# Linear attention with ReLU features: loads issued ahead of the stores in one DMA queue, larger runs, and one order of work to the end

## The chip, the core and the metric

The kernel runs on one NeuronCore of a Trainium2 chip. Five engines work side by side, each through its own queue in order: TensorE (PE) does matmuls and transposes into PSUM, VectorE (DVE) and ScalarE (ACT) do elementwise work, GpSimd (POOL) issues most DMA transfers here, and SyncE (SP) issues a few. Sixteen DMA engines move the data between HBM and the on-chip SBUF; each transfer is spread over all sixteen, and its semaphore is complete when the last of them has reported. The metric is the device time in microseconds (us) of one execution, the median over several. A profiled execution has a span, from its first instruction to its last, and a somewhat longer time.

## The reference

For each of 8 x 12 = 96 heads, with 512 positions and 64 dimensions, all in fp32:

```python
Q_feat = np.maximum(0, Q)
K_feat = np.maximum(0, K)
KV = np.einsum('bhkd,bhkv->bhdv', K_feat, V)        # 64 x 64 per head
K_sum = np.sum(K_feat, axis=2)
numerator = np.einsum('bhqd,bhdv->bhqv', Q_feat, KV)
denominator = np.einsum('bhqd,bhd->bhq', Q_feat, K_sum)
return numerator / (denominator[:, :, :, None] + 1e-10)
```

Q, K and V hold 12.58 MB each, and so does the result.

## The kernel before, in words

**Tiling.** Heads are taken eight at a time: an "octet" `o`, 12 in all (`NO`). An octet's Q, K, V and result are 1.05 MB each in HBM. K and V of an octet are cut into two groups of four heads, `g = 2*o` and `2*o+1`. Loads through GpSimd cast fp32 to bf16 on the way, so a load writes half of what it reads. Octet 0 comes another way: K and V in fp32 through SP and ACT (lines 124 and 125), Q through GpSimd.

**Buffers.** `k_all`, `v_all` and `q_all` are a ring of six octets (`RING = DELAY + 1 = 6`): octet `o` lies in slot `(o-1) % 6`. A load of octet `o + 6` therefore waits until octet `o` has been used: K by VectorE (line 195), V by VectorE and ScalarE (197, 204, 202), Q by TensorE's transposes (230). Results go into `o_sb`, seven rotating buffers, of which the fp32 K and V of octet 0 take the first two.

**GpSimd's queue.** GpSimd issues its transfers in program order, and a transfer whose wait is not met holds up those behind it. The compiler gives these transfers eight semaphores in turn, so each transfer also waits for the one eight places ahead to land. Before: octets 1 to 6 in three runs of two (`FIRST`), K, then V, then Q; then store 0, store 1, load 7, store 2, load 8, store 3 and so on to store 5, load 11, and stores 6 to 9. The load of octet `o + 6` follows the store of octet `o` in `store` (lines 309 to 311). From octet 9 on (`PAIRS`) K and V come by group, in halves. Stores 10 and 11 go through SP, the last in two halves (lines 301 to 305).

**Work per octet.** `prep(g)` (DVE, lines 195 and 197) and `prep_v` (204 on DVE, 202 on ACT) make ReLU(K) and V masked for their place. `mm_kv` (line 209) sums K-transposed V over 16 matmuls per group, and `evac_kv` (219) copies it to SBUF as `kvd`. `qt` transposes Q on TensorE (230) and applies ReLU (238). `denom` (269, 272, 277, 281) makes the reciprocal of the denominator; `out_t` (260, 262) the numerator, transposed; `back` (287) transposes it back, and `norm` (293) multiplies by the reciprocal into `o_sb`. `idle` (247) is a number of matmuls whose result nobody reads.

**Order of work.** The schedule is written by hand; each engine runs its instructions in the order of the program. For `o` from 0 to 8 an iteration is: K-V matmuls and evacuation of `o`, preparation of group `2o+2`, back and norm of `o-1`, denominators and output of `o`, preparation of `2o+3`, transposed Q of `o+1`. From octet 9 on the order changes: the K-V matmuls of `o+1` and the back of `o` are drawn into iteration `o` (lines 359 to 361), and the last two octets are written out in lines 363 to 388, with some of ScalarE's copies put on VectorE (`share`, and `relu_q` with `nc.vector`).

Of the kernel before, what the change touches and what calls it, by code (L numbers as in the profile page):

```python
# [10 lines left out]
def kernel(  # L11
# [7 lines left out]
    nc = tc.nc  # L19
    B, H, S, D = Q.shape  # L20
    assert D == 64
    P = 128
    D1 = D + 1
# [4 lines left out]
    RQ = S * 8 // P  # L28
    NHG = 4
    U = RQ // 2  # L30
    NG = NH // NHG
    NO = NG // 2
# [3 lines left out]
    fp32 = mybir.dt.float32  # L36
    bf16 = mybir.dt.bfloat16
    Act = mybir.ActivationFunctionType
# [23 lines left out]
    NK = 2  # L62
# [26 lines left out]

    q_sb, k_sb, v_sb = {}, {}, {}  # L90

    PAIRS = NO - 3
    RING = DELAY + 1
    FIRST = (2, 2, 2)
    k_all = consts.tile([P, 2 * RING, R, D], bf16, name="k_all")
    v_all = consts.tile([P, 2 * RING, R, D], bf16, name="v_all")
    q_all = consts.tile([P, RING + 1, U, 2 * D], bf16, name="q_all")
# [6 lines left out]

    def load_kv(X, tile_, first, n):
        to = 2 * ((first // 2 - 1) % RING) + first % 2
        if n == 1:
            nc.gpsimd.dma_start(out=tile_[:, to].rearrange("p r d -> p (r d)"), in_=X[first], single_packet=True)  # L108
            return
        nc.gpsimd.dma_start(out=tile_[:, to:to + n].rearrange("p n r d -> p n (r d)"),  # L110
                            in_=X[first:first + n].rearrange("n p f -> p n f"), single_packet=True)

# [13 lines left out]
    load_q(0)  # L126
    make_identity(nc, ident)

    def load_octet(o, n=1):
        m = 1 if o >= PAIRS else 2 * n  # L130
        for g in range(2 * o, 2 * (o + n), m):
            load_kv(Kr, k_all, g, m)
            load_kv(Vr, v_all, g, m)
        load_q(o, n)

    o = 1
    for n in FIRST:
        load_octet(o, n)
        o += n
    assert o == RING + 1  # L140

    def zero_masks():
        for h in range(NHG):
# [48 lines left out]
    def prep(g):  # L192
        kf[g] = kfp.tile([P, R, 2, D], bf16, name="kf")
        for s in range(2):
            nc.vector.tensor_scalar(kf[g][:, :, s, :], k_sb[g], scalar1=0.0,  # L195
                                    scalar2=mask[:, 0, s:s + 1], op0=Alu.max, op1=Alu.mult)
        nc.vector.tensor_scalar(vo[g % NB][:, :, 0, 2:D + 2], v_sb[g], scalar1=mask[:, 1, 0:1],  # L197
                                scalar2=None, op0=Alu.mult)

    def prep_v(g, eng):  # L200
        if eng is nc.scalar:
            nc.scalar.activation(vo[g % NB][:, :, 1, 2:D + 2], v_sb[g], Act.Copy, scale=mask[:, 1, 1:2])  # L202
        else:
            nc.vector.tensor_scalar(vo[g % NB][:, :, 1, 2:D + 2], v_sb[g], scalar1=mask[:, 1, 1:2],  # L204
                                    scalar2=None, op0=Alu.mult)

    def mm_kv(g):
        for r in range(R):
            nc.tensor.matmul(  # L209
                ps_kv[:, g % 2, 0:2 * (D + 2)].rearrange("p (t d) -> p t d", t=2),  # L210
                kf[g][:, r, :, :].rearrange("p s d -> p (s d)"), vo[g % NB][:, r, :, 1:D4 - 1],
                start=(r == 0), stop=(r == R - 1), skip_group_check=True)


    def evac_kv(o, gs, share=False):
        for s in range(2):
            for c in range(2):
                copy = nc.vector.tensor_copy if share and c == 1 else nc.scalar.copy
                copy(  # L219
                    kvd[o % NK][64 * c:64 * c + 64, 4 * gs.start + s:4 * gs.stop:2,  # L220
                               c * D1:c * D1 + D1].rearrange(
                        "p (g t) d -> p g t d", t=2),
                    ps_kv[64 * s:64 * s + 64, gs, 0:2 * (D + 2)].rearrange(
                        "p g (t d) -> p g t d", t=2)[:, :, :, c:c + D1])


    def transp(o, i):
        ps = pqt.tile([P, U // 2, P], bf16, name="ps_qt")
        for u in range(U // 2):
            nc.tensor.transpose(ps[:, u, :], q_sb[o][:, i * (U // 2) + u, :], ident)  # L230
        return ps

    def relu_q(o, i, ps, eng=None):
        to = qt_sb[o % NZ][:, i * (U // 2):(i + 1) * (U // 2)]
        if eng is nc.vector:
            nc.vector.tensor_scalar(to, ps, scalar1=0.0, scalar2=None, op0=Alu.max)
        else:
            nc.scalar.activation(to, ps, Act.Relu)  # L238

    def qt(o):  # L240
        for i in range(2):
            relu_q(o, i, transp(o, i))


    def idle(n, o):
        for i in range(n):
# [2 lines left out]

    def out_t(o, halves=range(2)):
        if halves[0] == 0:
            ot[o] = otp.tile([P, U, 8, 16], fp32, name="ot_sb")
        q = qt_sb[o % NZ].rearrange("p u (h c) -> p u h c", h=8)
        for j in halves:
# [9 lines left out]
    def denom(o):  # L266
        ps = ps_den[:, 0].rearrange("p (u h c) -> p u h c", u=U, h=8)
        for u in range(U):
            nc.tensor.matmul(ps[:, u], qt_sb[o % NZ][:, u, :], kvd[o % NK][:, :, 0:2 * D1:2 * D1 - 1],  # L269
                             start=True, stop=True, skip_group_check=True)  # L270
        own = rcp.tile([P, U, 8, 2], fp32, name="own")
        nc.vector.scalar_tensor_tensor(
            own.rearrange("p u h c -> p u (h c)"), ps.rearrange("p u h c -> p u (h c)"), 1e-10,
            mask_h.rearrange("p h c -> p (h c)").unsqueeze(1).to_broadcast([P, U, 16]),
            op0=Alu.add, op1=Alu.mult)
        den = rcp.tile([P, RQ], fp32, name="den")
        nc.vector.tensor_reduce(out=den.rearrange("p (u c) -> p u c", c=2),  # L277
                                in_=own.rearrange("p u h c -> p u c h"), op=Alu.add,
                                axis=mybir.AxisListType.X)
        rec[o] = rcp.tile([P, RQ], fp32, name="rec")  # L280
        nc.vector.reciprocal(rec[o], den)
# [15 lines left out]


    def store(o, o_sb):
        Ov = Or[o].rearrange("p (r d) -> p r d", d=D)  # L300
        if o == NO - 1:
            for j in range(2):
                rs = slice(RQ // 2 * j, RQ // 2 * (j + 1))
                nc.sync.dma_start(out=Ov[:, rs], in_=o_sb[:, rs])
            return
        if o >= NO - 2:
            nc.sync.dma_start(out=Ov, in_=o_sb)
            return
# [7 lines left out]
    both = slice(0, 2)  # L316
# [15 lines left out]
    def backs(o):  # L332
        o_sb = out_tile()
        for j in range(2):
            norm(o, j, back(o, j), o_sb)
        store(o, o_sb)

    def kvs(o):
        mm_kv(2 * o)
        mm_kv(2 * o + 1)  # L340
        evac_kv(o, both)

    SAME = NO - 4
    for o in range(NO - 2):
        if 0 < o <= SAME:
            kvs(o)
        prep(2 * o + 2)
        prep_v(2 * o + 2, nc.scalar)  # L350
        if 0 < o <= SAME:
            backs(o - 1)
        denom(o)
        out_t(o)
        prep(2 * o + 3)
        prep_v(2 * o + 3, nc.vector)
        if o >= SAME:
            kvs(o + 1)
        qt(o + 1)
        if o >= SAME:  # L360
            backs(o)

    o = NO - 2
    g = 2 * NO - 2
    prep(g)
    prep_v(g, nc.vector)
    denom(o)
    out_t(o)
    mm_kv(g)
    evac_kv(o + 1, slice(0, 1))  # L370
    prep(g + 1)
    prep_v(g + 1, nc.vector)

    o_sb = out_tile()
    norm(o, 0, back(o, 0), o_sb)
    ps = back(o, 1)
    mm_kv(g + 1)
    evac_kv(o + 1, slice(1, 2), share=True)
    for i in range(2):
        relu_q(o + 1, i, transp(o + 1, i), nc.vector if i == 1 else None)  # L380
    norm(o, 1, ps, o_sb)
    store(o, o_sb)
    idle(5, o + 1)
    out_t(o + 1, (0,))
    denom(o + 1)
    out_t(o + 1, (1,))
    idle(6, o + 1)
    backs(o + 1)
# [1 line left out]
_INS = ['Q', 'K', 'V']  # L390
_OUTS = [((8, 12, 512, 64), 'float32')]
# [25 lines left out]
```

## Time and profile before

| What | Value |
|---|---|
| median of 3 runs | 126.27 us (125.77, 126.27, 126.27) |
| the profiled execution's time | 126.86 us |
| its span | 125.1 us |
| TensorE matmul busy | 86.3 us, 69% of the span |
| VectorE busy | 83.2 us, 67% |
| ScalarE busy | 80.6 us, 64% |
| read from HBM, written | 37.75 MB, 12.58 MB |
| GpSimd's transfers: packets, share of 16 engines' span | 9104, 94.5% |

In the page's second part the span is cut into 40 slices of 3.1 us. A digit is the busy share of a slice in tenths; the DMA row is the mean over the sixteen DMA engines. GB/s counts what is written, so a casting load shows half of what it reads. A line of a timeline holds start, duration, engine, source line, operation, result and operands, and how many instructions stand in it; in brackets the idle time before it and what ended it. "Landing" times are the moments at which the DMA engines reported that their part of a transfer was done, in us from the span's start.

### The profile page before, as it was taken

What the parts mean: (1) busy time and instruction counts of PE and PEld (TensorE: products, weight loads), DVE (VectorE), ACT (ScalarE), POOL (GpSimd) and SP (SyncE); (2) the same over time, 40 slices, a digit from 0 to 9 for tenths busy, and PEclk for the clock granted to TensorE, in tenths of its full rate; (3) what the DMA queues carried; (4) which work ended last, traced back from release to release, by engine and by line L of the source; (5) the groups of instructions that cost most, each with busy time, mean ns of one, the idle gap of its engine ahead of it and who ended that gap; (6) DMA issues with size and microseconds to landing.
All of it is one profiled execution on the core that took longest, in us unless ns stands there. A gap on an engine that the chain in (4) does not pass through costs nothing.

```text
span 125.1 us, 2615 instructions
## 1 busy us (share of the span) xinstructions
PE 86.3 (69%) x1067; PEld 77.6 (62%) x1067; DVE 83.2 (67%) x192; ACT 80.6 (64%) x112; POOL 26.5 (21%) x47
## 2 busy tenths in 40 slices
PE   0005884089898998959989897799596496888500
PEld 0005563089787897839978786698494494876400
DVE  2719716920997979797297984967909819977700
ACT  0009966544989989896598988658669466646000
POOL 6942020000100901203311122144333321000000
PEclk9999999558999999995999999859999999999995
DMA  4999999999999999999999999999999999999991
GB/s 84 389 321 206 212 210 217 214 210 210 215 219 208 212 212 218 214 321 419 217 204 307 282 218 264 324 212 238 347 214 226 356 224 216 349 422 424 430 390 76
DMA packets 9836, 32.67 MB, mean 261 GB/s; under 512 B 736, under 2 KB 736, under 8 KB 8160
## 3 DMA queue, kind: packets, MB, share of 16 engines
q0 software_dynamic: 9104, 28.31, 94.5%
q1 hardware_dynamic: 576, 3.15, 6.6%
q10 hardware_dynamic: 144, 1.05, 2.2%
q8 instruction: 8, 0.13, 0.4%
q14 instruction: 4, 0.03, 0.1%
HBM read 37.75 MB, written 12.58 MB: 402 GB/s over the span
## 4 chain that ended last, share of the span: by engine, by line
DMA 44%; DVE 23%; PE 19%; POOL 4%; ACT 2%; issue 2%; DVEq 1%; POOLq 0%
DMA q_all<-in_Q_dram 28%; DMA v_all<-in_V_dram 16%; DVE o_sb L293 13%; PE ps_kv L209 8%; PE ps_bk L287 6%; PE ps_qt L230 3%; DVE kf L195 3%; ACT ot_sb L262 2%; DVE vo_all L197 2%; PE ps_ot L260 1%; DVE vo_all L204 1%; POOL k_all L110 1%; POOL v_all L110 1%; DVE den L277 1%; DVEq L412 1%
## 5 line engine op out<-in xcount | busy, mean ns | idle before, releaser
L293 DVE TENSOR_TENSOR o_sb<-ps_bk,rec 128x1024 f32<-128x1024 f32 x24 | 28.3, 1218 | 20.0 <-PE ps_bk L287 20.0
L209 PE MATMUL ps_kv<-vo_all,kf 128*128 128x132 bf16 x352 | 26.9, 238 | 4.9 <-DVE vo_all L204 4.4
L209 PEld LDWEIGHTS <-kf 128*128 128x128 bf16 x352 | 24.8, 106 | 6.2 <-issue 3.5
L230 PE MATMUL ps_qt<-ident,q_all 128*128 128x128 bf16 x192 | 15.5, 245 | 15.9 <-DMA q_all<-in_Q_dram 15.8
L262 ACT COPY ot_sb<-ps_ot 128x1024 f32<-128x1024 f32 x24 | 24.0, 1013 | 3.8 <-PE ps_ot L260 2.9
L219 ACT CAST kvd<-ps_kv 64x260 bf16<-64x260 f32 (+1 forms) x46 | 16.5, 359 | 15.1 <-PE ps_kv L209 13.9
L238 ACT ACTIVATE qt<-ps_qt 128x1024 bf16<-128x1024 bf16 x23 | 22.4, 1025 | 3.6 <-PE ps_qt L230 3.5
L230 PEld LDWEIGHTS <-q_all 128*128 128x128 bf16 x192 | 13.7, 111 | 16.9 <-DMA q_all<-in_Q_dram 16.7
L287 PE MATMUL ps_bk<-ident,ot_sb 128*128 128x128 f32 x192 | 23.0, 273 | 0.4 <-ACT ot_sb L262 0.4
L287 PEld LDWEIGHTS ps_bk<-ident,ot_sb 128*128 128x128 f32 x192 | 20.8, 142 | 0.7 <-ACT ot_sb L262 0.7
L195 DVE TENSOR_SCALAR kf<-k_all,mask 128x1024 bf16<-128x1024 bf16 x44 | 18.3, 458 | 1.4 <-DMA k_all<-in_K_dram 1.3
L260 PE MATMUL ps_ot<-qt,kvd 128*128 128x256 bf16 x96 | 13.9, 272 | 6.2 <-DVE o_sb L293 5.5
L260 PEld LDWEIGHTS <-kvd 128*128 128x128 bf16 x96 | 8.9, 97 | 8.8 <-issue 7.0
L309 POOL DMA_DIRECT2D out_dram<-o_sb x10 | 5.5, 551 | 39.8 <-DVE o_sb L293 31.0
L202 ACT ACTIVATE vo_all<-v_all,mask 128x1024 bf16<-128x1024 bf16 x10 | 11.5, 1154 | 1.3 <-DMA v_all<-in_V_dram 1.2
L197 DVE TENSOR_SCALAR vo_all<-v_all,mask 128x1024 bf16<-128x1024 bf16 x22 | 10.6, 483 | 2.1 <-DMA v_all<-in_V_dram 2.1
L269 PEld LDWEIGHTS <-qt 128*128 128x128 bf16 x192 | 6.7, 96 | 4.9 <-ACT qt L238 2.0
L269 PE MATMUL ps_den<-kvd,qt 128*128 128x16 bf16 x192 | 7.3, 179 | 3.0 <-ACT kvd L189 1.7
L178 ACT ACT_TABLE_LOAD x1 | 1.3, 1283 | 9.7 <-DMA v_first<-in_V_dram 9.7
L204 DVE TENSOR_SCALAR vo_all<-v_all,mask 128x1024 bf16<-128x1024 bf16 x12 | 5.8, 480 | 0.0
L110 POOL DMA_DIRECT2D v_all<-in_V_dram x5 | 4.0, 810 | 7.8 <-ACT ot_sb L262 4.4
L108 POOL DMA_DIRECT2D k_all<-in_K_dram x6 | 3.6, 604 | 8.4 <-DMA q_all<-in_Q_dram 4.9
(36 smaller groups left out, 56.7 us busy)
## 6 DMA issues: line engine op xcount, KB each, us to landing
out_dram<-o_sb POOLq DMA_DIRECT2D x10, 1024.0 KB, 15.2
q_all<-in_Q_dram POOLq DMA_DIRECT2D x6, 512.0 KB, 13.8
k_all<-in_K_dram POOLq DMA_DIRECT2D x3, 1024.0 KB, 26.9
v_all<-in_V_dram POOLq DMA_DIRECT2D x3, 1024.0 KB, 31.0
q_all<-in_Q_dram POOLq DMA_DIRECT2D x3, 1024.0 KB, 35.1
k_all<-in_K_dram POOLq DMA_DIRECT2D x6, 256.0 KB, 13.4
v_all<-in_V_dram POOLq DMA_DIRECT2D x6, 256.0 KB, 12.3
v_first<-in_V_dram ACTq DMA_DIRECT2D x1, 1024.0 KB, 8.9
```

Of the source, the lines that this page charges most:

```text
L195: nc.vector.tensor_scalar(kf[g][:, :, s, :], k_sb[g], scalar1=0.0, scalar2=mask[:, 0, s:s + 1], op0=Alu.max, op1=Alu.mult)
L197: nc.vector.tensor_scalar(vo[g % NB][:, :, 0, 2:D + 2], v_sb[g], scalar1=mask[:, 1, 0:1], scalar2=None, op0=Alu.mult)
L202: nc.scalar.activation(vo[g % NB][:, :, 1, 2:D + 2], v_sb[g], Act.Copy, scale=mask[:, 1, 1:2])
L209: nc.tensor.matmul(ps_kv[:, g % 2, 0:2 * (D + 2)].rearrange("p (t d) -> p t d", t=2), kf[g][:, r, :, :].rearrange("p s d -> p (s d)"), vo[ ...
L219: copy(kvd[o % NK][64 * c:64 * c + 64, 4 * gs.start + s:4 * gs.stop:2, c * D1:c * D1 + D1].rearrange("p (g t) d -> p g t d", t=2), ps_kv[6 ...
L230: nc.tensor.transpose(ps[:, u, :], q_sb[o][:, i * (U // 2) + u, :], ident)
L238: nc.scalar.activation(to, ps, Act.Relu)
L260: nc.tensor.matmul(ps[:, i], kvd[o % NK][:, h, 1:2 * D + 1], q[:, :, h, :], start=True, stop=True, skip_group_check=True)
L262: nc.scalar.copy(ot[o][:, :, 4 * j:4 * j + 4], ps.rearrange("p h u c -> p u h c"))
L269: nc.tensor.matmul(ps[:, u], qt_sb[o % NZ][:, u, :], kvd[o % NK][:, :, 0:2 * D1:2 * D1 - 1], start=True, stop=True, skip_group_check=True)
L287: nc.tensor.transpose(ps[:, 2 * v:2 * v + 2].rearrange("p c d -> p (c d)"), ot[o][:, 8 * j + v].rearrange("p h c -> p (h c)"), ident32)
L293: nc.vector.tensor_tensor(o_sb[:, rs], ps, rec[o][:, rs].unsqueeze(2).to_broadcast([P, 16, D]), op=Alu.mult)
```

## The change

GpSimd's queue is written as a plan. Octets 1 to 11 come in runs of 3, 3, 2, 2 and 1 (`RUNS`); a run is one transfer each of K, V and Q, and K and V are no longer cut by group at the end. A load is put as far ahead of the stores as `HEAD = 4` allows, which gives this order: load 1-3, load 4-6, load 7-8, store 0, load 9-10, store 1, load 11, stores 2 to 9. `pump` puts the next entries of the plan into the queue as soon as the program has passed what they need. A load still waits until the old content of its slots has been used: 7-8 for octets 1 and 2, 9-10 for octets 3 and 4, 11 for octet 5.

The order of work is that of the first nine iterations through all twelve octets; the written-out end is gone, and with it `share` and the ReLU on VectorE. Five idle matmuls stand before the denominators of octet 11 and six before its back transposes, as before in number. The store of octet 11 goes through SP in one piece. TensorE has as many instructions as before, VectorE four fewer, ScalarE one more.

```diff
-    PAIRS = NO - 3
     RING = DELAY + 1
-    FIRST = (2, 2, 2)
+    RUNS = (3, 3, 2, 2, 1)
...
-    def load_octet(o, n=1):
-        m = 1 if o >= PAIRS else 2 * n
-        for g in range(2 * o, 2 * (o + n), m):
-            load_kv(Kr, k_all, g, m)
-            load_kv(Vr, v_all, g, m)
+    def load_octets(o, n):
+        load_kv(Kr, k_all, 2 * o, 2 * n)
+        load_kv(Vr, v_all, 2 * o, 2 * n)
         load_q(o, n)
-    o = 1
-    for n in FIRST:
-        load_octet(o, n)
+    HEAD = 4
+    plan, o, done = [], 1, 0
+    for n in RUNS:
+        last = o + n - 1 - RING
+        while done < last - HEAD + 1:
+            plan.append(("store", done, done))
+            done += 1
+        plan.append(("load", o, n))
         o += n
-    assert o == RING + 1
+    plan += [("store", i, i) for i in range(done, NO - 2)]
+    ready = {}
+    def pump(done):
+        while plan:
+            kind, o, n = plan[0]
+            if kind == "load" and o + n - 1 - RING <= done:
+                load_octets(o, n)
+            elif kind == "store" and o in ready:
+                nc.gpsimd.dma_start(out=Or[o].rearrange("p (r d) -> p r d", d=D), in_=ready[o], single_packet=True)
+            else:
+                return
+            plan.pop(0)
+    pump(0)
...
     def store(o, o_sb):
-        Ov = Or[o].rearrange("p (r d) -> p r d", d=D)
-        if o == NO - 1:
-            for j in range(2):
-                rs = slice(RQ // 2 * j, RQ // 2 * (j + 1))
-                nc.sync.dma_start(out=Ov[:, rs], in_=o_sb[:, rs])
-            return
         if o >= NO - 2:
-            nc.sync.dma_start(out=Ov, in_=o_sb)
-            return
-        nc.gpsimd.dma_start(out=Ov, in_=o_sb, single_packet=True)
-        if 0 < o < NO - RING:
-            load_octet(o + RING)
+            nc.sync.dma_start(out=Or[o].rearrange("p (r d) -> p r d", d=D), in_=o_sb)
+        else:
+            ready[o] = o_sb
...
+    for o in range(NO):
+        if o > 0:
+            kvs(o)
+        if o + 1 < NO:
+            prep(2 * o + 2)
+            prep_v(2 * o + 2, nc.scalar)
+        if o > 0:
+            backs(o - 1)
+        if o + 1 == NO:
+            idle(5, o)
         denom(o)
         out_t(o)
...
+        if o + 1 < NO:
+            prep(2 * o + 3)
+            prep_v(2 * o + 3, nc.vector)
+            qt(o + 1)
+        pump(o + 1)
+    idle(6, NO - 1)
+    backs(NO - 1)
```

More of the change, by code (lines that the diff above doesn't have):

```diff
@@ L106, in load_kv @@
         to = 2 * ((first // 2 - 1) % RING) + first % 2
-        if n == 1:
-            nc.gpsimd.dma_start(out=tile_[:, to].rearrange("p r d -> p (r d)"), in_=X[first], single_packet=True)
-            return
         nc.gpsimd.dma_start(out=tile_[:, to:to + n].rearrange("p n r d -> p n (r d)"),
@@ L127 @@
     make_identity(nc, ident)
-    def load_octet(o, n=1):
-        m = 1 if o >= PAIRS else 2 * n
-        for g in range(2 * o, 2 * (o + n), m):
-            load_kv(Kr, k_all, g, m)
-            load_kv(Vr, v_all, g, m)
-        load_q(o, n)
-    o = 1
-    for n in FIRST:
-        load_octet(o, n)
-        o += n
-    assert o == RING + 1
+    def load_octets(o, n):
+        load_kv(Kr, k_all, 2 * o, 2 * n)
+        load_kv(Vr, v_all, 2 * o, 2 * n)
+        load_q(o, n)
+    HEAD = 4
[6 more added lines that the diff above has]
+        plan.append(("load", o, n))
+        o += n
+    plan += [("store", i, i) for i in range(done, NO - 2)]
+    assert o == NO
+    ready = {}
[10 more added lines that the diff above has]
+    pump(0)
     def zero_masks():
@@ L212, in mm_kv, with evac_kv @@
                 start=(r == 0), stop=(r == R - 1), skip_group_check=True)
-    def evac_kv(o, gs, share=False):
+    def evac_kv(o):
         for s in range(2):
             for c in range(2):
[L218 to L221, printed above, removed]
+                nc.scalar.copy(
+                    kvd[o % NK][64 * c:64 * c + 64, s::2, c * D1:c * D1 + D1].rearrange(
                         "p (g t) d -> p g t d", t=2),
-                    ps_kv[64 * s:64 * s + 64, gs, 0:2 * (D + 2)].rearrange(
+                    ps_kv[64 * s:64 * s + 64, :, 0:2 * (D + 2)].rearrange(
                         "p g (t d) -> p g t d", t=2)[:, :, :, c:c + D1])
@@ L231, in transp @@
         return ps
[L233 to L238, printed above, removed]
     def qt(o):
         for i in range(2):
-            relu_q(o, i, transp(o, i))
+            nc.scalar.activation(qt_sb[o % NZ][:, i * (U // 2):(i + 1) * (U // 2)], transp(o, i), Act.Relu)
     def idle(n, o):
@@ L248, in idle, with out_t @@
                              skip_group_check=True)
-    def out_t(o, halves=range(2)):
-        if halves[0] == 0:
-            ot[o] = otp.tile([P, U, 8, 16], fp32, name="ot_sb")
+    def out_t(o):
+        ot[o] = otp.tile([P, U, 8, 16], fp32, name="ot_sb")
         q = qt_sb[o % NZ].rearrange("p u (h c) -> p u h c", h=8)
-        for j in halves:
+        for j in range(2):
             ps = pou.tile([P, 4, U, 16], fp32, name="ps_ot", tag="ps_out")
@@ L299, in store @@
     def store(o, o_sb):
-        Ov = Or[o].rearrange("p (r d) -> p r d", d=D)
-        if o == NO - 1:
-            for j in range(2):
-                rs = slice(RQ // 2 * j, RQ // 2 * (j + 1))
-                nc.sync.dma_start(out=Ov[:, rs], in_=o_sb[:, rs])
-            return
-        if o >= NO - 2:
-            nc.sync.dma_start(out=Ov, in_=o_sb)
-            return
-        nc.gpsimd.dma_start(out=Ov, in_=o_sb, single_packet=True)
-        if 0 < o < NO - RING:
-            load_octet(o + RING)
+        if o >= NO - 2:
+            nc.sync.dma_start(out=Or[o].rearrange("p (r d) -> p r d", d=D), in_=o_sb)
+        else:
+            ready[o] = o_sb
     def out_tile():
         return outp.tile([P, RQ, D], fp32, name="o_sb", tag="o_sb")
-    both = slice(0, 2)
     zero8()
@@ L340, in kvs @@
         mm_kv(2 * o + 1)
[L341 to L347, printed above, removed]
+        evac_kv(o)
+    for o in range(NO):
+        if o > 0:
             kvs(o)
-        prep(2 * o + 2)
-        prep_v(2 * o + 2, nc.scalar)
-        if 0 < o <= SAME:
+        if o + 1 < NO:
+            prep(2 * o + 2)
+            prep_v(2 * o + 2, nc.scalar)
+        if o > 0:
             backs(o - 1)
+        if o + 1 == NO:
+            idle(5, o)
         denom(o)
         out_t(o)
[L355 to L388, printed above, removed]
+        if o + 1 < NO:
[5 more added lines that the diff above has]
+    backs(NO - 1)
+    assert not plan
 _INS = ['Q', 'K', 'V']
```

## The prediction

> **What bounds the kernel now.** I read the table of busy slices first, then the sums over stretches, the order of instructions on TensorE, and last the times at which each transfer reported from its 16 DMA engines. In the busy slices the DMA row stands at 9 almost throughout, while no compute engine passes 69% of the span.
>
> ```profile
> span 125.1 us, 2615 instructions
> PE 86.3 (69%) x1067; PEld 77.6 (62%) x1067; DVE 83.2 (67%) x192; ACT 80.6 (64%) x112; POOL 26.5 (21%) x47
> ...
> DMA  4999999999999999999999999999999999999991
> ...
> q0 software_dynamic: 9104, 28.31, 94.5%
> ...
> HBM read 37.75 MB, written 12.58 MB: 402 GB/s over the span
> ```
>
> The GB/s of a stretch count the bytes that are written. K, V and Q are cast from 4 to 2 bytes on the way, so 215 GB/s of a load is 430 GB/s read, the same as the 426 GB/s of stores. In these stretches the last two numbers are DMA share and GB/s, the one before them the granted TensorE clock:
>
> ```profile
> 12.50:15.00 2.50, 1.90 (x11) 1.20 (x9) 2.45 (x4) 2.50 (x3) 0.00 (x0) 1.00 1.13 215
> ...
> 27.50:30.00 2.50, 2.50 (x32) 2.50 (x31) 0.00 (x0) 1.08 (x2) 0.00 (x0) 0.66 1.11 212
> ...
> 112.50:115.00 2.50, 2.29 (x30) 1.78 (x30) 2.31 (x4) 1.68 (x2) 0.00 (x0) 1.00 1.01 426
> ...
> 120.00:122.50 2.50, 0.00 (x0) 0.00 (x0) 0.00 (x0) 0.00 (x0) 0.00 (x0) 0.77 0.84 346
> 122.50:125.00 2.50, 0.00 (x0) 0.00 (x0) 0.00 (x0) 0.00 (x0) 0.00 (x0) 0.50 0.12 49
> ```
>
> So one stream of transfers runs without a gap. The landings say how it ends. Of each transfer I take the first and the last of its 16 engines: Q of octet 0 at 10.44 and 10.68; Q of octets 1 and 2 at 25.27 and 25.52; Q of 5 and 6 at 54.84 and 56.16; Q of 11 at 106.94 and 109.28; the last half store at 121.71 and 124.16. By its quickest engine the stream needs 121.71 - 10.44 = 111.27 us after octet 0; its slowest engine lags 2.45 us at the end. This lag grew in two steps: from 0.25 to 1.29 about 29.2, where a 16 KB instruction fetch runs, and from 1.12 to 2.23 about 62, where packets that usually take 0.17 us took up to 1.24.
>
> Compute is the second limit. Undisturbed, one octet takes 7.09 us (the back transposes start at 30.05, 37.14, 44.23 and 51.33), against about 9.9 us of DMA for its 3 MB read and 1 MB written.
>
> ```profile
> 25.57 1.89 PE L230 MATMUL ps_qt<-ident,q_all 128*128 128x128 bf16 x16 [4.30 <-DMA q_all<-in_Q_dram]
> 27.25 2.96 PE L209 MATMUL ps_kv<-vo_all,kf 128*128 128x132 bf16 x32
> 30.05 1.92 PE L287 MATMUL ps_bk<-ident,ot_sb 128*128 128x128 f32 x16
> ...
> 37.14 1.91 PE L287 MATMUL ps_bk<-ident,ot_sb 128*128 128x128 f32 x16
> ...
> 44.23 1.91 PE L287 MATMUL ps_bk<-ident,ot_sb 128*128 128x128 f32 x16
> ...
> 48.16 1.06 PE L230 MATMUL ps_qt<-ident,q_all 128*128 128x128 bf16 x16
> ...
> 51.33 1.91 PE L287 MATMUL ps_bk<-ident,ot_sb 128*128 128x128 f32 x16
> ```
>
> **The change, part by part.** *Bytes and transfers.* Not a byte is saved. GpSimd issues 26 transfers instead of 41 (6 of Q, 5 each of K and V, 10 stores, for 9, 11, 11 and 10), SP one store instead of two halves. What a transfer costs beyond its bytes shows in the landings. Octet 8's four transfers (69.67 to 79.55) take 9.88 us; octets 9 and 10, cut into six for the same bytes, 9.92 each; octet 11, also six, 10.03. That is 0.02 to 0.075 us per extra transfer. Octet 8's K and V together (4.93) equal one two-octet transfer (4.93), so zero is possible too. Bounds for 15 fewer: 0 and 1.1 us; I take 15 x 0.02 = 0.30 saved, as two of the three rows say. The last store whole: each engine moves 8 packets of 8 KB at 0.309 us instead of 16 of 4 KB at 0.159, so 2.47 for 2.54: 0.07 saved.
>
> *Loads ahead of stores.* This pays only if stores between loads slow the stream. Octet 8's mix of three loads and a store moves 4.19 MB in 9.88 us, 2.356 us per MB; the eight transfers of 2.10 MB that land from 20.39 to 54.84 with no store between, in 39.44 us after 15.40, need 2.351. Bounds 0 and 0.2 us over ten octets; I take 0.
>
> *Larger first runs.* Octets 1 to 3 now come as three transfers of 3.15 MB, and nothing of Q 1 to 3 can be used before its whole. One octet's K, V or Q, 1.05 MB in HBM, takes 2.467 us (nine two-octet transfers from 10.44 to 54.84, 4.933 each), so it lands at 10.44 + 9 x 2.467 = 32.6, with lag 32.9, instead of 25.5. TensorE's queue has the transposes of octet 1 at its head, so everything behind waits 7.4 us longer. The transposes went out 0.05 us after the landing, and the back transposes of octet 0 4.48 us after that, already at half clock (0.50 to 29.19), so a longer idle time makes no colder start: back(0) at 37.4.
> Of this the trace shows the wait; the Trainium skill ("DMA: Bandwidth & Descriptors", "Why a DMA increments its semaphore by 16 and not by 1") says that only the full count means that all has landed, which speaks against large runs. The wait above agrees.
>
> *New waits on GpSimd's queue.* K 7-8 reuses the slots of octets 1 and 2 and waits for VectorE's preparation of octet 2, 6.0 us after back(0) (30.05 to 36.06): 43.4. Behind it stand V, Q, store 0 and the rest, but the DMA engines have work until Q 4-6 at 54.8: 11 us of cover. K 9-10 waits for octet 4, 14.2 us later: 57.6, needed at 72.1 (54.84 + 6 x 2.467 + 2.45 for store 0). Load 11 waits for octet 5 about 64.7 and, Q last, for Q 7-8 at 71.8; needed at 89. Stores 2 to 8 then wait on the transfer eight places ahead, as now; store 9 is ready about 105 and due about 114. All these waits cost nothing. Were the cover gone, each us would lengthen the stream by one.
>
> *Output buffers.* There are seven; norm(9) (102 to 103) needs the one of store 2, which lands about 99.2 + 2.3 = 101.5. Cover 0.5 to 1.5 us; a us beyond it would go into the chain below.
>
> *Steady order to the end.* Octet 11's eight half-size evacuations (six on ScalarE at about 0.28, two on VectorE at 0.30) become four on ScalarE, 1.57 together as in every iteration; a Relu (0.69) and a preparation (0.48) move from VectorE to ScalarE, where they take 1.02 and 1.15. All this is part of the 7.09 us of a full iteration, so it costs nothing beyond it. Chain: back(0) 37.4, back(2) 51.6. Q of octet 4 is wanted 3.93 us later (44.23 to 48.16), at 55.5, but lands with Q 4-6 at 56.16: 0.65 lost. After that every load is early (Q 11 at 99 for 106). Back(10) at 37.4 + 70.9 + 0.65 = 109.0. Then 1.91 us of back transposes, 0.71 of idle matmuls and 0.58 of denominators bring the first output matmul to 112.2; from there to the last normalisation the old tail took 112.55 to 118.89. Last store issued at 118.5.
>
> *Where they meet.* The first packet of the old last store came 1.07 us after its issue (117.78 to 118.85), so the new one's is due at 119.6. The engines finish the store before it at 118.8 (quickest) to 121.3 (slowest). The slowest engine, which sets the end, has no gap, and the chain may slip 1.7 us more at no cost.
>
> **Sum.** 125.1 - 0.30 - 0.07 = 124.7 us of span. The profiled execution took 126.86, 1.8 beside its span, and stands 0.59 above the median of 126.27. Taken off the median, 0.37 gives 125.9.
>
> **Rivals.** *Faster, through the lag.* The second step of the lag, 1.11 us, comes as load K 7 follows stores 0 and 1 back to back. That order occurs nowhere in the new queue, where single stores stand between loads (single stores later show no step). If the order made it, it goes: 0.37 + 1.0 off, 124.9. Against it: the quickest engine showed nothing then, and a passing disturbance would look the same. The upper price per transfer (1.1 + 0.07) gives 125.1 by another way.
> By the Trainium skill ("DMA: Bandwidth & Descriptors", "Anatomy of one DMA") a transfer has a fixed cost of about 2 us; 15 fewer would be 30 us if they stood in line. By the rows above, with eight of them in flight, it is at most 0.075 each.
>
> *Slower, through the late start.* Octets 1 to 11 are now one unbroken chain on TensorE, VectorE and ScalarE from 32.9 to 118.5, where the old kernel caught up in its waits for data. It decides once the last store is issued after 120.2 (slowest engine free at 121.3, less 1.07). An iteration of 7.4 instead of 7.09 is enough: 3.1 us more, the store at 121.6, 1.4 late, 127.3. For it: half-clock stretches (at 57 and 81) lengthened the way from the transposes to the back transposes to 4.4 us (56.21 to 60.60) from 2.9 (41.32 to 44.23). Against it: those followed waits for data, which the new order has only once.
>
> *No change in the stream* is my forecast itself: the loads' place does nothing, only the overhead shrinks.
>
> **Numbers.** Forecast 0.47 (125.9, own range 125.6 to 126.9: the three runs shown differ by 0.5); faster through lag or transfer cost 0.32 (124.9 to 125.6); slower through the late start 0.21 (126.9 to 128). Half a per cent, 0.63 us, is about what a measurement can tell. The range leaves a tenth at either end: 125.0 to 127.3. Chances: faster 0.32, same 0.47, slower 0.21.
>
> **What would show it.** DMA row at 9 to the end; TensorE's first wait for Q ends about 33; back transposes every 7.09 us with one short wait for Q 4-6 about 56; last store on SP about 118.5; the lag of the last landing near 2.4, or near 1.4 if the rival is right. A fall of the DMA row about 55, 72 or 119 to 121 would show me wrong: a queue run dry, or a late chain.

## The result

The changed kernel takes 125.84 us (median of 22 runs, 125.66 to 126.35); the kernel before, run beside it, 126.27 us (22 runs, 125.77 to 127.51). The ratio is 0.9965, with a 95% interval of 0.995 to 0.9979: 0.43 us faster, which is clear of the noise but below the half per cent that the prediction named as about what a measurement can tell. The forecast was 125.9 us. The runs of the changed kernel also lie closer together, 0.7 us from the shortest to the longest against 1.7. All ratios in this document leave out runs that took over 1.5% longer than the shortest of their kernel; that concerns two kernels below, old_queue (three of twelve runs) and old_end (two of six).

The profiled execution has a span of 124.2 us and a time of 126.15. Its page answers to the lines shown of before: the DMA row again stands at 9 to the end, and the engines' shares have hardly moved. ScalarE has 112 instructions in both pages; the one more that was announced with the change is not there.

```profile
span 124.2 us, 2593 instructions
PE 83.1 (67%) x1067; PEld 75.5 (61%) x1067; DVE 81.8 (66%) x188; ACT 82.5 (66%) x112; POOL 18.3 (15%) x32
...
DMA  3999999999999999999999999999999999999993
...
q0 software_dynamic: 8864, 28.31, 94.7%
...
HBM read 37.75 MB, written 12.58 MB: 405 GB/s over the span
```

The sums over stretches of the changed kernel (last three numbers: granted TensorE clock, DMA share, GB/s written) show the same rates as before, 215 for loads and 426 for stores, at the same places. The difference stands in the last row: after 122.5 us hardly anything moves any more, 10 GB/s for 49.

```profile
12.50:15.00 2.50, 1.91 (x12) 1.29 (x10) 2.50 (x5) 2.50 (x3) 0.00 (x0) 1.00 1.13 215
27.50:30.00 2.50, 0.00 (x0) 0.00 (x0) 2.50 (x8) 1.51 (x2) 0.00 (x0) 0.50 1.06 215
112.50:115.00 2.50, 1.76 (x17) 1.18 (x13) 1.73 (x4) 1.90 (x2) 0.00 (x0) 1.00 1.01 426
120.00:122.50 2.50, 0.00 (x0) 0.00 (x0) 0.00 (x0) 0.00 (x0) 0.00 (x0) 0.66 0.85 357
122.50:125.00 2.50, 0.00 (x0) 0.00 (x0) 0.00 (x0) 0.00 (x0) 0.00 (x0) 0.50 0.02 10
```

TensorE's order in time is the other view that was shown. The transposes of octet 1 (line 245, before 230) now wait for Q 1-3 until 33.3 us, and from the second octet on the back transposes (line 293, before 287) come every 7.09 to 7.14 us with no wait for data to the very end:

```profile
33.31 1.89 PE L245 MATMUL ps_qt<-ident,q_all 128*128 128x128 bf16 x16 [12.11 <-DMA q_all<-in_Q_dram]
34.99 3.73 PE L226 MATMUL ps_kv<-vo_all,kf 128*128 128x132 bf16 x32
38.51 2.10 PE L293 MATMUL ps_bk<-ident,ot_sb 128*128 128x128 f32 x16
...
45.79 1.91 PE L293 MATMUL ps_bk<-ident,ot_sb 128*128 128x128 f32 x16
...
52.89 1.92 PE L293 MATMUL ps_bk<-ident,ot_sb 128*128 128x128 f32 x16
...
56.81 1.06 PE L245 MATMUL ps_qt<-ident,q_all 128*128 128x128 bf16 x16
...
102.60 1.91 PE L293 MATMUL ps_bk<-ident,ot_sb 128*128 128x128 f32 x16
...
109.69 1.92 PE L293 MATMUL ps_bk<-ident,ot_sb 128*128 128x128 f32 x16
```

The chain of waits that ended last has turned over with this: before, DMA had the largest share (44%), now VectorE has (40%), and one landing of Q is all that is left of DMA. That reads as if the kernel were now bound by compute. The DMA row says otherwise, and the experiments below decide it: the chain ends with the last store, which both limits reach within a microsecond of each other. First before, then changed:

```profile
DMA 44%; DVE 23%; PE 19%; POOL 4%; ACT 2%; issue 2%; DVEq 1%; POOLq 0%
```

```profile
DVE 40%; PE 24%; DMA 23%; issue 3%; POOL 2%; DVEq 1%; ACT 1%; ACTq 1%; POOLq 0%
```

### The profile page after: what moved, and what is told of

It reads as the page before. It is cut to its first block, busy times and chain, and to the rows that moved or that the text cites. A ratio compares the mean times of both kernels' runs of the same rounds, so it can differ in the third digit from the quotient of the medians.

```text
span 124.2 us, 2593 instructions
## 1 busy us (share of the span) xinstructions
PE 83.1 (67%) x1067; PEld 75.5 (61%) x1067; DVE 81.8 (66%) x188; ACT 82.5 (66%) x112; POOL 18.3 (15%) x32
## 4 chain that ended last, share of the span: by engine, by line
DVE 40%; PE 24%; DMA 23%; issue 3%; POOL 2%; DVEq 1%; ACT 1%; ACTq 1%; POOLq 0%
DMA q_all<-in_Q_dram 23%; DVE o_sb L299 20%; PE ps_kv L226 12%; PE ps_bk L293 10%; DVE kf L212 5%; DVE den L283 3%; DVE vo_all L221 3%; DVE vo_all L214 3%; DVE rec L287 3%; DVE own L278 3%; PE ps_qt L245 2%; DVEq L385 1%; ACT ot_sb L268 1%; ACTq L385 1%; POOL v_all L106 1%
## 5 line engine op out<-in xcount | busy, mean ns | idle before, releaser
L245 PE MATMUL ps_qt<-ident,q_all 128*128 128x128 bf16 x192 | 14.3, 235 | 23.2 <-DMA q_all<-in_Q_dram 23.2
L226 PE MATMUL ps_kv<-vo_all,kf 128*128 128x132 bf16 x352 | 25.9, 231 | 2.3 <-DVE vo_all L221 2.3
L245 PEld LDWEIGHTS <-q_all 128*128 128x128 bf16 x192 | 13.0, 106 | 23.7 <-DMA q_all<-in_Q_dram 23.4
L250 ACT ACTIVATE qt<-ps_qt 128x1024 bf16<-128x1024 bf16 x24 | 23.3, 1027 | 5.4 <-PE ps_qt L245 5.4
L226 PEld LDWEIGHTS <-kf 128*128 128x128 bf16 x352 | 23.2, 102 | 3.6 <-issue 3.6
L235 ACT CAST kvd<-ps_kv 64x260 bf16<-64x260 f32 x44 | 16.5, 374 | 7.0 <-PE ps_kv L226 6.2
L219 ACT ACTIVATE vo_all<-v_all,mask 128x1024 bf16<-128x1024 bf16 x11 | 12.7, 1154 | 6.5 <-DMA v_all<-in_V_dram 6.2
L283 DVE TENSOR_REDUCE den<-own 128x32 f32<-128x256 f32 x12 | 5.0, 420 | 0.4
```

The lines of the kernel that those rows point to most:

```text
L226: nc.tensor.matmul(ps_kv[:, g % 2, 0:2 * (D + 2)].rearrange("p (t d) -> p t d", t=2), kf[g][:, r, :, :].rearrange("p s d -> p (s d)"), vo[ ...
L235: nc.scalar.copy(kvd[o % NK][64 * c:64 * c + 64, s::2, c * D1:c * D1 + D1].rearrange("p (g t) d -> p g t d", t=2), ps_kv[64 * s:64 * s + 6 ...
L250: nc.scalar.activation(qt_sb[o % NZ][:, i * (U // 2):(i + 1) * (U // 2)], transp(o, i), Act.Relu)
```

## The experiments

Theory: the sixteen DMA engines work without a gap, and the slowest of them sets the end. The changed order of work costs nothing because the last store still reaches the queue before that engine is free. The gain is a little less work per engine (fewer transfers) and a smaller lag of the slowest. Rivals: the order in GpSimd's queue made the gain, above all that stores 0 and 1 no longer stand together; the steady order of work made it; the late start of the chain costs something. All ratios are against the kernel before, run beside each.

For each profile I use four landings: the first transfer's first engine (Q of octet 0), the store of octet 10's first and last engine, and the last landing of all. The lag of a transfer is the time from its first to its last landing. "Mean" is the time from Q 0 to store 10 as the mean over all sixteen engines; over the five profiles with the changed kernel's number of transfers it varies by 0.14 us, the time of the quickest engine by 0.26.

| Profile | Q 0, first | store 10, first and last | between the firsts | mean | lag | last landing |
|---|---|---|---|---|---|---|
| before, three profiles | 10.44, 10.44, 10.30 | 119.21/121.72, 119.16/121.01, 118.97/121.23 | 108.77, 108.72, 108.67 | 109.77, 109.53, 109.52 | 2.5, 1.9, 2.3 | 124.16, 123.48, 123.69 |
| changed, two profiles | 10.16, 10.31 | 118.86/120.90, 119.01/120.54 | 108.70, 108.70 | 109.37, 109.30 | 2.0, 1.5 | 123.33, 122.95 |
| split_all | 10.20 | 119.41/121.13 | 109.21 | 109.97 | 1.7 | 123.73 |
| stores_together | 10.40 | 118.84/120.45 | 108.44 | 109.23 | 1.6 | 122.88 |
| runs_of_two | 10.39 | 118.82/120.42 | 108.43 | 109.21 | 1.6 | 123.13 |
| late1 | 10.23 | 118.76/120.34 | 108.53 | 109.30 | 1.6 | 123.13 |
| late3 | 10.32 | 118.98/121.13 | 108.66 | 109.30 | 2.2 | 123.77 |

**The changed kernel again, and the kernel before twice more.**

> The changed kernel as it is, as the measure for the other kernels of this row and for a second profile: 0.9965 of the kernel before, within 0.002; last landing about 123.3 in its span, lag of the last but one store near 2.

> The kernel before as it is, for a second profile. If the lag's second step about 62 us belongs to this kernel, six or more DMA engines step back 0.8 us there again. If it was a passing disturbance, the lag stays near 1.3 to 1.6 from octet 6 to the end and the last landing comes about 1 us earlier than in the first profile, at 123.2.

> The same once more, for a third profile: the step about 62 again, or not.

The changed kernel again took 125.79 us, 0.9976 (0.9959 to 0.9994) of the kernel before. The three profiles of the kernel before differ mainly in the lag: 2.5, 1.9 and 2.3 us at the store of octet 10, against 2.0 and 1.5 in the changed kernel. Its second step, near 62 us while load K 7 runs, appears in all three, but at 1.1 us only in the first; in the others it is 0.3 and 0.5 (lag of store 1 and of load K 7: 1.12 and 2.23, 1.61 and 1.88, 1.50 and 1.96), where two packets took up to 0.66 us and not six up to 1.24. Stores show a smaller lag than the loads beside them; counted from load Q 5-6 ahead of the two stores (1.32, 1.76 and 1.78) to load K 7, the steps are 0.9, 0.1 and 0.2. So most of the step that I read was a passing disturbance. Whether the small rest belongs to that kernel was not found out.

**Every transfer cut up.**

```diff
-        load_kv(Kr, k_all, 2 * o, 2 * n)
-        load_kv(Vr, v_all, 2 * o, 2 * n)
-        load_q(o, n)
+        for X, to in ((Kr, k_all), (Vr, v_all)):
+            for g in range(2 * o, 2 * (o + n)):
+                load_kv(X, to, g, 1)
+        for i in range(o, o + n):
+            load_q(i)
```

> Edit: the changed kernel, but every run's K and V go group by group and its Q octet by octet, 55 loads instead of 16. Same bytes, same order. If a transfer costs 0.02 us beyond its bytes, as the octets 8 to 10 of the kernel before say: 39 x 0.02 = 0.8 us slower than the changed kernel, about 126.6. If it costs 0.075 (octet 11): 2.9 us slower, 128.8. If it costs nothing and the gain came from the order of the queue alone: 125.8, no change. Octet 1's Q lands about 27.7 instead of 32.4, so the chain of compute starts earlier; on my theory that is worth nothing.

126.59 us, 1.0001 (0.9975 to 1.0027): the gain is gone. From Q 0 to store 10 the quickest DMA engine needs 109.21 us where the changed kernel needs 108.70, and the mean of the sixteen 109.97 where the five profiles with the changed kernel's number of transfers (changed, stores_together, late1, late3) have 109.30 on average, from 109.23 to 109.37. For 39 transfers that is 0.51 or 0.67 us, 0.013 or 0.017 each. It is a little below the 0.02 that the forecast took, and 15 transfers come to 0.2 to 0.26 us instead of 0.30.

**The first two stores together.**

```diff
-    HEAD = 4
+    HEAD = 3
```

> Edit: HEAD = 3, so store 0 and store 1 stand back to back in front of load 9-10, and store 2 in front of load 11. If two stores in a row ahead of a load delay several DMA engines (the second step of the lag in the kernel before), the last landing lags 1 us more and the time is 126.4 to 126.9, with a wider spread. If that step was a passing disturbance: 125.8, and the lag after the two stores stays near 2.0 us.

125.99 us, 0.9956 (0.9937 to 0.9975): as quick as the changed kernel. The lag, 1.54 at load Q 7-8, is 1.64 and 1.43 at the two stores and 1.63 at K 9-10 behind them. From load to load, across the two stores in a row, that is a step of 0.1 us and not of 1; that rival falls.

**The last store later.** Two kernels, with 18 and 33 idle matmuls instead of 6 in front of the last back transposes (the index of their operand taken modulo 8):

```diff
-    idle(6, NO - 1)
+    idle(18, NO - 1)
```

> Edit: 18 idle matmuls instead of 6 in front of the last back transposes; the first 0.65 us of them is wait time already, so the last store is issued about 1.0 us later, at 119.6. Theory: the slowest DMA engine is busy with the store before it until about 120.9, and the first packet comes 1.07 us after the issue, at 120.7; no change, 125.8. Rival (the last store is what ends the kernel): 126.8.

> Edit: 33 idle matmuls instead of 6 in front of the last back transposes, the last store about 3.0 us later, at 121.6, first packet at 122.6. Theory: 1.3 us of the delay are free (slowest engine busy until 120.9, first packet of the undelayed store at 119.6), so 1.7 us slower, 127.5. Rival (no slack): 3.0 slower, 128.8. Rival (the quick engines' gap counts as well, slack over 2 us): 126.5 or less.

125.91 us, 0.9959 (0.9936 to 0.9981), and 126.75 us, 1.0021 (0.9996 to 1.0046). The first delay is free, the second costs 0.8 us beside the first, less than the 1.7 expected: the store was issued only 1.3 us later than in the changed kernel and not 3.0. Of the difference 0.8 us is a chain that ran earlier in that profile for another reason (below), and the rest is idle matmuls, which put the last back transposes off by 2.1 us (3.60 from their start instead of 1.47) where 3.0 were expected. The issues and landings give a rule without that uncertainty. Issue, first and last landing of the last store:

```
                 issue    first landing   last landing   issue to first
changed          118.59       122.27         123.33           3.68
changed again    118.66       122.34         122.95           3.68
late1            119.27       122.96         123.13           3.69
late3            119.90       123.58         123.77           3.68
```

A quick engine delivers its part 3.68 us after the issue, and where all sixteen are free the last follows at 3.86. The slowest engine delivers 2.43 us after its part of store 10 (120.90 to 123.33). The end is the later of the two. For the changed kernel they are 122.45 and 123.33: the slowest engine decides. For late1 they are 123.13 and 122.77, for late3 123.76 and 123.56: there the store's issue decides, and the lag of the last landing shrinks to 0.17 and 0.19. The rule is good to some 0.3 us: in runs_of_two below the slowest engine took 2.71 us for its last part (120.42 to 123.13). The changed kernel has 0.9 us to spare in one profile and 0.4 in the other. In the stretches of the third kernel the drained engines can be seen, 175 GB/s in the first row where the changed kernel moves 393. First the changed kernel, then late3:

```profile
119.00:120.50 1.50, 0.00 (x0) 0.00 (x0) 0.00 (x0) 0.00 (x0) 0.00 (x0) 1.00 0.93 393
120.50:121.50 1.00, 0.00 (x0) 0.00 (x0) 0.00 (x0) 0.00 (x0) 0.00 (x0) 0.65 1.04 434
121.50:122.50 1.00, 0.00 (x0) 0.00 (x0) 0.00 (x0) 0.00 (x0) 0.00 (x0) 0.50 0.57 238
122.50:123.50 1.00, 0.00 (x0) 0.00 (x0) 0.00 (x0) 0.00 (x0) 0.00 (x0) 0.50 0.06 25
```

```profile
119.00:120.50 1.50, 0.00 (x0) 0.00 (x0) 0.88 (x1) 0.00 (x0) 0.00 (x0) 1.00 0.42 175
120.50:121.50 1.00, 0.00 (x0) 0.00 (x0) 0.00 (x0) 0.00 (x0) 0.00 (x0) 1.00 0.92 385
121.50:122.50 1.00, 0.00 (x0) 0.00 (x0) 0.00 (x0) 0.00 (x0) 0.00 (x0) 0.86 0.98 401
122.50:124.00 1.50, 0.00 (x0) 0.00 (x0) 0.00 (x0) 0.00 (x0) 0.00 (x0) 0.50 0.43 175
```

**One half of the change alone.** First the old queue with the steady order of work:

```diff
-    SAME = NO - 4
-    for o in range(NO - 2):
...
+    for o in range(NO):
+        if o > 0:
+            kvs(o)
...
+    idle(6, NO - 1)
+    backs(NO - 1)
```

> Edit: the kernel before with its queue, its transfers and its last store in halves, but with the steady order of work to the end. Q of octet 11 lands about 109.3, and from its transposes to the last store's issue the changed kernel takes 12.04 us (106.52 to 118.56), so the second half is issued about 121.4 and the first 1.15 earlier. A whole store needs 3.9 us from issue to its last landing, so the first half lands by 122.9 and the second by 124.1, beside the slowest DMA engine at 124.2. Theory (slowest engine and last store, whichever is later): within 0.4 us of the kernel before. Rival (chain of compute decides): 1 to 2.5 us slower than the kernel before.

1.0037 (1.0004 to 1.0071), 0.5 us slower than the kernel before, with runs from 125.9 to 128.2 us. The halves are issued at 121.15 and 122.27, each 0.9 us later than expected, and the last landing is at 125.06 with a lag of 0.18: the store's issue decides, which is nearer to the rival. Store 10 too came late (issued 116.84, first landing 120.54 where the kernel before has 119.21). This profile is of an execution of 127.73 us, 0.8 above the median of the twelve runs, so in a median run the store is issued earlier.

TensorE's order shows where the 0.9 us arose. Behind the old queue the transposes of octet 11 wait for their data, the granted clock is 0.50 from 108.70 to 112.12, and from these transposes to the back transposes behind them it takes 4.13 us; the changed kernel takes 3.17 (106.52 to 109.69) at full clock. From there to the issue of the last transfer both take 8.9 us. So the 0.9 us beyond the expectation stand where the clock was halved, and the order's own length added nothing to them. What the steady order costs behind the old queue without such a stretch was not measured.

```profile
109.25 1.89 PE L230 MATMUL ps_qt<-ident,q_all 128*128 128x128 bf16 x16 [1.66 <-DMA q_all<-in_Q_dram]
110.93 2.61 PE L209 MATMUL ps_kv<-vo_all,kf 128*128 128x132 bf16 x32
113.38 1.92 PE L287 MATMUL ps_bk<-ident,ot_sb 128*128 128x128 f32 x16
```

Then the new queue and whole last store with the old order in the last four octets:

```diff
-    for o in range(NO):
-        if o > 0:
-            kvs(o)
...
+    SAME = NO - 4
+    for o in range(NO - 2):
+        if 0 < o <= SAME:
+            kvs(o)
...
+        pump(o + 1)
```

> Edit: the changed kernel's queue, runs and whole last store, but the kernel before's order of work in the last four octets. Theory: the stream of transfers is the same and the slowest DMA engine sets the end, so the time is that of the changed kernel within 0.2 us. Rival (the steady order brought the gain): the time of the kernel before, 0.4 slower. If the old order is longer without waits for data, the last store is issued later than 119.5 and it is slower by as much as it is later.

1.0236 (1.0184 to 1.0289), with runs from 128.5 to 131.9 us: the slowest kernel of all, and the expectation's last case. Its last store is issued at 121.87 in the profile, with its first landing 3.68 later. TensorE's order of this kernel shows why: in the old order an octet takes 9.18 us even with all its data there (denominators at 97.47 and 106.65, no wait for DMA between them), where the steady order takes 7.09. In it the back transposes come behind the transposes of Q. VectorE stands idle 2.97 us for them, its norm goes ahead of the next preparation, and the K-V matmuls then wait 0.47 and 1.54 us for that preparation (`vo_all`). TensorE's order first, then two lines of VectorE's:

```profile
95.43 1.92 PE L304 MATMUL ps_bk<-ident,ot_sb 128*128 128x128 f32 x16
97.47 0.38 PE L286 MATMUL ps_den<-kvd,qt 128*128 128x16 bf16 x8
98.38 0.38 PE L286 MATMUL ps_den<-kvd,qt 128*128 128x16 bf16 x8 [0.54 <-ACT qt L255]
98.61 1.03 PE L277 MATMUL ps_ot<-qt,kvd 128*128 128x256 bf16 x8
100.11 1.12 PE L226 MATMUL ps_kv<-vo_all,kf 128*128 128x132 bf16 x16 [0.47 <-DVE vo_all L214]
102.77 1.11 PE L226 MATMUL ps_kv<-vo_all,kf 128*128 128x132 bf16 x16 [1.54 <-DVE vo_all L221]
...
104.61 1.92 PE L304 MATMUL ps_bk<-ident,ot_sb 128*128 128x128 f32 x16
106.65 0.38 PE L286 MATMUL ps_den<-kvd,qt 128*128 128x16 bf16 x8
```

```profile
96.51 2.35 DVE L310 TENSOR_TENSOR o_sb<-ps_bk,rec 128x1024 f32<-128x1024 f32 x2 [2.97 <-PE ps_bk L304]
98.78 0.87 DVE L212 TENSOR_SCALAR kf<-k_all,mask 128x1024 bf16<-128x1024 bf16 x2
```

Neither half does what the two do together. The old order was made for data that arrive 10 us apart; behind a queue that has the data early it is the bound.

**That kernel once more.** Its runs spread, so it was profiled a second time.


> The changed kernel's queue with the old order in the last four octets once more, since its executions spread from 128.5 to 131.9 and the profiled one was among the shortest. Theory: the last store is issued late (121.8 in the first profile) because an octet takes 9.2 us in the old order, and the kernel ends 3.9 us after that issue; a longer execution shows a later issue by as much. Rival: the last store itself takes longer than 3.9 us.

This execution took 131.06 us, with the last store issued at 124.36 and its first landing again 3.68 us later: all of the difference to the first profile lies in the chain. Two pieces make its 2.49 us. TensorE's first stretch of half clock lasted to 38.72 instead of 36.55, so the first back transposes began at 38.71 instead of 37.53, 1.18 later, of which 1.00 is left at those of 96.43 (95.43). The other 1.49 come with a second stretch of half clock in the chain, between 103.6 and 107.0 (clock 0.51 in the second row; the rates in the last column are those of stores throughout). In it the K-V matmuls of line 226 took 1.92 us for 1.11. This holds for the one execution; the other long ones have no profile.

```profile
100.00:103.50 3.50, 1.76 (x22) 1.37 (x21) 3.43 (x10) 2.23 (x3) 0.61 (x1) 1.00 1.02 426
103.50:107.00 3.50, 3.23 (x31) 3.23 (x31) 0.22 (x1) 1.15 (x4) 0.00 (x0) 0.51 1.01 421
107.00:110.50 3.50, 3.04 (x40) 2.72 (x39) 2.32 (x3) 2.51 (x4) 0.00 (x0) 1.00 1.02 431
```

**The chain started earlier.**

```diff
-    RUNS = (3, 3, 2, 2, 1)
+    RUNS = (2, 2, 2, 2, 2, 1)
```

> Edit: RUNS = (2, 2, 2, 2, 2, 1) instead of (3, 3, 2, 2, 1); three transfers more, the same place of the stores. Q of octet 1 lands about 25.3 instead of 32.4, so the chain of compute starts 7 us earlier, but waits more for later data. Theory: the slowest DMA engine sets the end, not the chain; no change against the changed kernel but 3 x 0.016 = 0.05 us, so 0.997 of the kernel before. Rival (the late start costs something): faster than the changed kernel by 0.3 us or more.

126.09 us, 0.999 (0.9966 to 1.0015): no faster than the changed kernel, whose ratios lie inside this interval or at its edge. The last store is issued at 117.09, 1.5 us earlier than in the changed kernel, and the last landing is at 123.13, between its two. The large first runs cost nothing, because the last store waits for the DMA engines anyway.

**A try at the slowest engines.** Since they end the kernel, one kernel gave eight engines more of store 10 and eight less:

```diff
-        if o >= NO - 2:
+        if o == NO - 2:
+            Ov = Or[o].rearrange("p (r d) -> p r d", d=D)
+            nc.sync.dma_start(out=Ov[0:96], in_=o_sb[0:96])
+            for p in range(96, P, 8):
+                nc.sync.dma_start(out=Ov[p:p + 8], in_=o_sb[p:p + 8])
+        elif o >= NO - 2:
```

> Edit: the store of octet 10 goes as one transfer of 96 partitions and four of 8 partitions. Theory: the slowest DMA engines end the kernel, about 1 us after the quick ones that then wait for the last store. If the transfers of 8 partitions go to eight of the sixteen engines, those carry 10 rows of the store and the others 6 instead of 8 each, 2 x 0.31 us more and less. If the slow engines are among the relieved ones, the last landing comes 0.5 us earlier (0.996 of the changed kernel); if they are among the loaded ones, 0.6 later. If all sixteen share the small transfers, no change.

126.81 us, 1.005 (1.0029 to 1.007), slower than both. Each small transfer reported from eight engines, as thought, but the four held SP's queue from 112.85 to 118.89, and the last store behind them was issued at 118.94, about a microsecond after its data were ready. Its last landing was at 124.30, beyond the 122.8 that its issue allows, so engines decided that were still at work on store 10. The extra load need not be the only reason: between 116.7 and 121 us 19 of SP's 8 KB packets took 0.44 to 1.26 us where 0.31 is usual. Which engines are the slow ones, and whether relieving them would gain, stays open.

None of the kernels tried is clearly faster than the changed one.

## Why the prediction was right, point by point

**The bound.** Right. The stream of transfers fills the time from 10 to 119 us in every kernel with the new queue and the steady order, at the same rate within 0.8%, and its slowest engine sets the end as long as the last store is issued in time.

**Fewer transfers.** Right in kind, a little too large. The term was 0.30 us at 0.02 each; split_all measures 0.013 to 0.017, so 0.2 to 0.26 us. The profiles of the two kernels agree: in the mean over the sixteen engines 109.53 and 109.52 us in the two of before that have no disturbance, 109.30 in the five with the changed queue's number of transfers, 0.2 us less. On the quickest engine alone the difference drowns: a mean of 108.72 us in the three of before, 108.70 in both of the changed kernel, while four other kernels with nearly the same transfers have 108.43 to 108.66.

**The lag.** The forecast left the lag at 2.45 us and put its shrinking into a rival. In the profiles the slowest engine finished store 10 at 121.72, 121.01 and 121.23 before and 120.90 and 120.54 after, 0.6 us earlier in the mean. But the 2.45 held a disturbance that came again in neither of the other two profiles of that kernel, and without it the lags of store 10 overlap: 1.9 and 2.3 before, 2.0 and 1.5 after, 1.6, 1.6 and 2.2 in the other kernels with the same number of transfers. So it isn't shown that the change made the lag smaller, and the rival's cause, two stores in a row, is out. That the sum of 0.37 came so near the 0.43 measured is in part luck: transfers and last store as measured come to 0.24 to 0.30, at the lower edge of the interval of the measurement (0.27 to 0.63 us). What made the rest, if there is one, stays open.

**The whole last store.** No run tried it alone. The landings show about half of its 0.07 us: from store 10 to the end the slowest engine took 2.44, 2.47 and 2.46 us for two halves before and 2.43 and 2.41 for the whole store after, 0.04 less in the mean.

**Larger first runs.** Right in effect. Q 1-3 landed at 32.38 to 33.26 (32.6 to 32.9 forecast). The back transposes began at 38.51 instead of 37.4: the forecast took over the half clock of the old trace, 3.6 us from the start of the matmuls, where in this execution it lasted until 38.89. The chain then met no wait for Q 4-6, for which 0.65 us had been set; it came to that point at 56.81, just after the landing at 56.67. At the back transposes of octet 10 the chain was 0.7 us late (109.69, forecast 109.0), and from there to the last store's issue it took 8.9 us for the 9.5 forecast. So it is luck that these errors nearly cancel: issued at 118.59, forecast 118.5.

**The waits in GpSimd's queue.** Right. The order in time of GpSimd in the changed kernel has loads K 7-8, K 9-10, K 11 and store 9 at 44.30, 58.50, 65.59 and 106.33 (43.4, 57.6, 64.7 and about 105 forecast), each far ahead of the stream:

```profile
44.30 0.80 POOL L106 DMA_DIRECT2D k_all<-in_K_dram  x1 [37.01 <-DVE kf L212]
...
58.50 0.79 POOL L106 DMA_DIRECT2D k_all<-in_K_dram  x1 [11.16 <-DVE kf L212]
...
65.59 0.70 POOL L106 DMA_DIRECT2D k_all<-in_K_dram  x1 [4.07 <-DVE kf L212]
...
106.33 0.53 POOL L152 DMA_DIRECT2D out_dram<-o_sb  x1 [6.57 <-DVE o_sb L299]
```

Norm(9) began at 103.68, 2.6 us after store 2 had landed (101.12): the buffers held nobody up.

**Where they meet.** The rule was right, its slack too large: 1.7 us forecast, 0.9 and 0.4 measured. The forecast counted from the first packet to the moment when the slowest engine is free. What counts is the 3.86 us from issue to the last landing against the slowest engine's end, and that engine was free at 120.9, not 121.3. The rival of the late chain was thus closer than it seemed; old_end shows what it does.

## What to carry to other kernels

In this kernel DMA is busy from end to end, and there 39 more transfers cost its stream 0.5 to 0.7 us, and another order of them nothing that these runs could resolve. In such a case compare the end of the slowest DMA engine with the issue of the last store plus its time to land, and only the later of the two is worth work. Queue order and order of work belong together: the order that suits late data cost 2.6% behind a queue that brings them early (1.0236 against 0.9976), and the steady order 0.4% behind the old queue (0.04 to 0.7%, with half clock in its profile). Repeat a profile before a single step in it becomes a cause.

## What the runs showed that had not been expected

The end of TensorE's first stretch of half clock varies from execution to execution by a microsecond and more, and the chain of compute with it. The clock records have half clock from 21.82 to 38.89 in the changed kernel's profile and from 23.23 to 36.88 in late3's, with the same work: 17.07 and 13.65 us, five and four pieces of 3.413 us. In the first the K-V matmuls of octet 1 took 3.73 us, in late3 2.87, and there the chain came to the back transposes of octet 10 0.8 us earlier (108.93 for 109.69). The Trainium skill ("TensorE: Matmul & The Clock Gate", "What's actually happening") says that the clock is judged in free-running windows of 3413 ns, which do not start with the kernel; the lengths in these traces agree. In the changed kernel, whose end is set by the DMA engines, the runs lie within 0.7 us; those of old_end, whose end is set by the chain, lie 3.3 us apart, and in its two profiled executions the difference goes with the clock.

Eight 16 KB instruction fetches run in each profile of the two kernels, each a packet of 0.88 to 0.98 us on one DMA engine. In the first profile of the kernel before, one more of the sixteen engines' landings falls about 1.0 to 1.3 us behind the first after the fetch at 29.2 (lag 0.25 to 1.28), then a second after that at 40.1 and a third after that at 51.3. In all five profiles the lag grows by 0.9 to 1.2 us with the first fetch and, the disturbance near 62 us aside, by 0.5 us at most with a later one; those mostly set back other engines. With the spread that is there from the start (0.2 to 0.85 us at Q 0) this makes up most of the lag in the changed kernel.
